# Sliding windows: most loads on GpSimd's queue, tiles cleared by ScalarE, four half-batch stores first

## Chip, cores, metric

One core of one Trainium2 chip. The metric is the device time of one execution in microseconds. The kernel before takes 195.61 us (median of 4 runs).

## The reference

The input x is float32 of shape (16, 64, 64, 64): batch, channels, height, width. Every 8 x 8 window at a stride of 4 is copied out, with all its channels.

```python
n_h = (h - window_size) // stride + 1      # 15
n_w = (w - window_size) // stride + 1      # 15
for i in range(n_h):
    for j in range(n_w):
        result[:, i, j] = x[:, :, i*4 : i*4 + 8, j*4 : j*4 + 8]
```

The output has 16 x 15 x 15 = 3600 rows of 64 x 8 x 8 floats, 16 KB each: 58.98 MB written for 16.78 MB read, and no arithmetic at all.

## The kernel before

A partition of the input tile L holds one band of 16 image rows of one image and of half of the channels: partition = 64 ch + 32 y + 4 b + q, with ch the half of the channels, y the half of the batch, b the image in that half and q the band. A load brings one (ch, y, q): 8 partitions, four apart, each with 32 channels x 4 KB. VectorE and ScalarE gather windows from L into one of four tiles G of 128 output rows, and GpSimd scatters a tile to the output with row numbers from an index tile. Numbers out of range skip a row: a "half store" has the rows of one half of the batch (64), a "whole" store 128, a "crossing" store (windows across two bands) 112.

```python
    L = lpool.tile([P, CL, RB, W], f32)
    x_v = x.rearrange("(y b) (ch cl) (hq r) w -> ch y hq b cl (r w)", y=NY, ch=CH, hq=HQ)
    SMALL = 4

    def load(eng, ch, y, q, c0, c1):
        p0 = ch * HP + y * QP + q
        eng.dma_start(out=L[p0 : p0 + QP - HQ + 1 : HQ, c0:c1, :, :], in_=x_v[ch, y, q, :, c0:c1, :])

# ... index tiles idx, idx_y0, idx_y1, idx_lo, idx_hi (VectorE, small) ...

    for y in range(NY):
        for q in range(HQ):
            load(nc.sync, 0, y, q, SMALL, CL)
            load(nc.gpsimd, 0, y, q, 0, SMALL)
            load(nc.gpsimd, 1, y, q, 0, CL)

# ...
    NG = 4
    G = [gpool.tile([P, C, WS, WS], f32, name=f"G{n}") for n in range(NG)]

# ... scatter(g, ix, j, s): indirect store of tile g; fill(g, half, s, j, lo, n, copies): gathers windows ...

    act, dve = nc.scalar.copy, nc.vector.tensor_copy

    EARLY = 3
    assert EARLY < NG
    for t in range(NG):
        for half in range(CH):
            p0 = half * HP + (QP if t < EARLY else 0)
            nc.vector.memset(G[t][p0 : p0 + QP, :, :, :], 0.0)
    t = 0
    for y in range(NY):
        for j in range(EARLY):
            for half in range(CH):
                copies = (dve, dve) if y and half and j == 1 else (act, dve)
                fill(G[t % NG], half, half, j, y * QP, QP, copies)
            scatter(G[t % NG], (idx_y0, idx_y1)[y], j, 0)
            t += 1

    units = [(j, s) for j in range(NW) for s in (0, 2) if s or j >= EARLY]
    for j, s in units:
        g = G[t % NG]
        t += 1
        if s == 0:
            for half in range(CH):
                fill(g, half, s + half, j, 0, HP, (act, dve))
            scatter(g, idx, j, s)
        else:

            turn = j % 2
            fill(g, turn, s, j, 0, HP, (act, act))
            fill(g, 1 - turn, s + 1, j, 0, HP, (dve, dve))
            scatter(g, (idx_hi, idx_lo)[turn], j, s)
```

## Time and profile before

| | before |
|---|---|
| median of 3 runs beside the profile | 195.66 us (195.56 to 195.69) |
| span of the profile | 193.9 us |
| DMA rate while loading / in the steady state | 401 / 421 GB/s |
| last 4 KB load packet ends (packet records) | 47.22 us |
| last output packet ends (packet records) | 190.60 us |

The prediction shows the views it rests on. One more is needed to read the change: the page's table of DMA queues (queue and kind: packets, MB, share of the 16 engines' span).

```profile
q0 software_dynamic: 9616, 68.43, 85.9%
q1 hardware_dynamic: 1856, 7.34, 9.8%
```

The software queue is GpSimd's, the hardware queue is SyncE's. SyncE loads 7.34 MB of the 16.78 MB; of GpSimd's 68.43 MB, 9.44 MB are loads.

### The profile page before, as it was taken

The page shows a single profiled execution, that of the slowest core. Times are in us where ns is not written, and L with a number is a line of the kernel's source. Part 1 is how long each engine was busy: PE and PEld are TensorE (multiplying, and loading weights), DVE is VectorE, ACT ScalarE, POOL GpSimd, SP SyncE. Part 2 cuts the span into 40 slices and gives each one's busy share as a digit, 9 for nine tenths or more (in the row PEclk, how much of TensorE's full clock was granted, in tenths as well). Part 3 has the DMA queues.
Part 4 walks back from the last instruction along what each step waited for, and adds up shares of the span by engine and source line. Part 5 has one row for each costly group of instructions (what it writes and reads, how often), then busy time and mean ns, then how long its engine had stood idle before and what let it go on. Part 6 is the DMA issues. An engine that isn't in the chain of part 4 may idle for free.

```text
span 193.9 us, 478 instructions
## 1 busy us (share of the span) xinstructions
DVE 131.9 (68%) x156; ACT 123.5 (64%) x66; POOL 53.3 (27%) x54
## 2 busy tenths in 40 slices
DVE  6887778995999998766577657774777477643000
ACT  0000008960999999999779677977797779772000
POOL 7402211106463233231404211331323232311000
DMA  2999999999989999999999999999999999999980
GB/s 85 326 408 401 402 399 397 400 400 405 426 333 382 406 419 419 423 423 404 426 433 421 416 419 419 423 423 433 423 416 412 426 423 423 426 416 421 412 345 30
DMA packets 11476, 75.81 MB, mean 391 GB/s; under 512 B 3776, under 2 KB 3776, under 8 KB 7872
## 3 DMA queue, kind: packets, MB, share of 16 engines
q0 software_dynamic: 9616, 68.43, 85.9%
q1 hardware_dynamic: 1856, 7.34, 9.8%
q14 instruction: 4, 0.03, 0.0%
HBM read 16.78 MB, written 69.21 MB: 444 GB/s over the span
## 4 chain that ended last, share of the span: by engine, by line
DMA 66%; DVE 17%; issue 6%; POOL 2%; POOLq 1%; DVEq 0%; PEldq 0%
DMA out_dram<-G,idx 21%; DMA L<-in_x_dram 18%; DMA out_dram<-G,idx_hi 14%; DMA out_dram<-G,idx_lo 12%; DVE G L136 8%; DVE G L139 6%; DVE G L138 3%; POOL L L57 2%; POOLq L204 1%; DVEq L136 0%; POOL pi L68 0%; DVEq L138 0%; PEldq L204 0%
## 5 line engine op out<-in xcount | busy, mean ns | idle before, releaser
L136 ACT COPY G<-L 64x2048 f32<-64x2048 f32 (+1 forms) x65 | 122.2, 1896 | 22.5 <-DMA out_dram<-G,idx 9.9
L136 DVE COPY G<-L 64x2048 f32<-64x2048 f32 (+1 forms) x37 | 44.8, 1221 | 15.6 <-DMA out_dram<-G,idx 12.7
L139 DVE STREAM_SHUFFLE G<-L 64x1024 f32<-64x1024 f32 x30 | 38.3, 1275 | 0.0
L138 DVE COPY G<-L 64x1024 f32<-64x1024 f32 x30 | 20.7, 690 | 20.1 <-DMA out_dram<-G,idx_hi 13.3
L150 DVE MEMSET G<- 32x4096 f32 x8 | 27.8, 3472 | 7.9 <-issue 6.2
L115 POOL DMA_INDIRECT out_dram<-G,idx x12 | 12.4, 1030 | 33.3 <-ACT G L136 33.3
L115 POOL DMA_INDIRECT out_dram<-G,idx_hi x8 | 11.8, 1471 | 31.4 <-DVE G L139 17.8
L136 ACT ACT_TABLE_LOAD x1 | 1.3, 1283 | 29.6 <-DMA L<-in_x_dram 29.6
L57 POOL DMA_DIRECT2D L<-in_x_dram x16 | 9.8, 626 | 25.0 <-DMA L<-in_x_dram 24.4
L115 POOL DMA_INDIRECT out_dram<-G,idx_lo x7 | 9.7, 1390 | 20.5 <-ACT G L136 14.3
L115 POOL DMA_INDIRECT out_dram<-G,idx_y x6 | 9.3, 1547 | 13.7 <-DVE G L136 8.8
L77 DVE TENSOR_TENSOR th<-tc,tq 128x1 int32<-128x1 int32 x2 | 0.3, 159 | 0.1
L77 DVE CUSTOM_DVE_ANT_0 idx_y<-idx,th 128x2 uint16<-128x2 uint16 x2 | 0.3, 158 | 0.1
L74 DVE TENSOR_SCALAR th<-tc 128x1 int32<-128x1 int32 x2 | 0.3, 154 | 0.1
L68 POOL IOTA pi<- 128x1 int32 x1 | 0.1, 125 | 0.4 <-PEq L204 0.4
L139 DVE LOAD_MASK_SELECT G<-L x30 | 0.2, 6 | 0.0
L77 DVE CUSTOM_DVE_ANT_0 idx_hi<-idx,th 128x2 uint16<-128x2 uint16 x1 | 0.2, 159 | 0.0
L77 DVE CUSTOM_DVE_ANT_0 idx_lo<-tb,th 128x2 uint16<-128x2 uint16 x1 | 0.2, 159 | 0.0
L77 DVE CUSTOM_DVE_ANT_0 idx<-tb,th 128x2 uint16<-128x2 uint16 x1 | 0.2, 161 | 0.0
L77 DVE CUSTOM_DVE_ANT_0 idx_lo<-idx_lo,th 128x2 uint16<-128x2 uint16 x1 | 0.2, 158 | 0.0
L77 DVE CUSTOM_DVE_ANT_0 tb<-tb,th 128x2 uint16<-128x2 uint16 x1 | 0.2, 159 | 0.0
L91 DVE TENSOR_SCALAR th<-th 128x1 int32<-128x1 int32 x1 | 0.2, 153 | 0.0
(13 smaller groups left out, 1.7 us busy)
## 6 DMA issues: line engine op xcount, KB each, us to landing
L<-in_x_dram POOLq DMA_DIRECT2D x8, 1024.0 KB, 21.1
L<-in_x_dram SPq DMA_DIRECT2D x8, 896.0 KB
L<-in_x_dram POOLq DMA_DIRECT2D x8, 128.0 KB, 21.3
out_dram<-G,idx POOLq DMA_INDIRECT x12, 14.6
out_dram<-G,idx_hi POOLq DMA_INDIRECT x8, 13.9
out_dram<-G,idx_lo POOLq DMA_INDIRECT x7, 14.1
out_dram<-G,idx_y POOLq DMA_INDIRECT x6, 6.2
```

Source lines behind the costliest of these rows:

```text
L57: eng.dma_start(out=L[p0 : p0 + QP - HQ + 1 : HQ, c0:c1, :, :], in_=x_v[ch, y, q, :, c0:c1, :])
L68: nc.gpsimd.iota(pi[:, :], pattern=[[0, 1]], base=0, channel_multiplier=1)
L74: nc.vector.tensor_scalar(out=d[:, :], in0=a[:, :], scalar1=float(m), scalar2=None, op0=ALU.mult)
L77: nc.vector.tensor_tensor(out=d[:, :], in0=a[:, :], in1=b[:, :], op=op)
L91: nc.vector.tensor_scalar(out=th[:, :], in0=th[:, :], scalar1=-1.0, scalar2=FAR, op0=ALU.mult, op1=ALU.add)
L115: st = nc.gpsimd.indirect_dma_start(out=o_v, out_offset=bass.IndirectOffsetOnAxis(ap=ix[:, 0:1], axis=0), in_=g.rearrange("p c r w -> p (c ...
L136: copy(out=g[d, cs, :, :], in_=L[f, :, s * ST : s * ST + WS, cols])
L138: copy(out=g[d, cs, 0:ST, :], in_=L[f, :, s * ST : RB, cols])
L139: nc.vector.stream_shuffle(out=g[d, cs, ST:WS, :], in_=L[f, :, 0:ST, cols], mask=nxt)
L150: nc.vector.memset(G[t][p0 : p0 + QP, :, :, :], 0.0)
L204: with _tile.TileContext(nc) as tc:
```

## The change

The intent: with most loads in one queue, the first half of the batch arrives before the second half begins, so that four half stores (one in each tile) can stand in the queue behind the loads. These give 10 us in which the second half of the batch is made ready, and whole stores between its half stores keep the queue full. ScalarE clears the tiles, because it has nothing else to do then.

```diff
--- before.py
+++ after.py
@@ -50,7 +50,8 @@
     x_v = x.rearrange("(y b) (ch cl) (hq r) w -> ch y hq b cl (r w)", y=NY, ch=CH, hq=HQ)
 
 
-    SMALL = 4
+
+    SMALL, HWP = 4, 2
 
     def load(eng, ch, y, q, c0, c1):
         p0 = ch * HP + y * QP + q
@@ -102,8 +103,10 @@
 
     for y in range(NY):
         for q in range(HQ):
-            load(nc.sync, 0, y, q, SMALL, CL)
-            load(nc.gpsimd, 0, y, q, 0, SMALL)
+            hw = y * HQ + q < HWP
+            if hw:
+                load(nc.sync, 0, y, q, SMALL, CL)
+            load(nc.gpsimd, 0, y, q, 0, SMALL if hw else CL)
             load(nc.gpsimd, 1, y, q, 0, CL)
 
     o_v = out.rearrange("b i j c r w -> (b i j) (c r w)")
@@ -142,35 +145,53 @@
 
 
 
-    EARLY = 3
-    assert EARLY < NG
-    for t in range(NG):
+    EARLY = NG
+    zero = ipool.tile([P, 1], f32, name="zero")
+    nc.vector.memset(zero[:, :], 0.0)
+    for g in G:
+        act(out=g.rearrange("p c r w -> p (c r w)"), in_=zero.to_broadcast([P, CFREE]))
+    at = 0
+
+    def tile_():
+        nonlocal at
+        at += 1
+        return G[(at - 1) % NG]
+
+    def part(y, j):
+        g = tile_()
         for half in range(CH):
-            p0 = half * HP + (QP if t < EARLY else 0)
-            nc.vector.memset(G[t][p0 : p0 + QP, :, :, :], 0.0)
-    t = 0
-    for y in range(NY):
-        for j in range(EARLY):
-            for half in range(CH):
-                copies = (dve, dve) if y and half and j == 1 else (act, dve)
-                fill(G[t % NG], half, half, j, y * QP, QP, copies)
-            scatter(G[t % NG], (idx_y0, idx_y1)[y], j, 0)
-            t += 1
-
-    units = [(j, s) for j in range(NW) for s in (0, 2) if s or j >= EARLY]
-    for j, s in units:
-        g = G[t % NG]
-        t += 1
+            fill(g, half, half, j, y * QP, QP, (dve, dve) if y and half else (act, dve))
+        scatter(g, (idx_y0, idx_y1)[y], j, 0)
+
+    crossed = 0
+
+    def unit(j, s):
+        nonlocal crossed
+        g = tile_()
         if s == 0:
             for half in range(CH):
-                fill(g, half, s + half, j, 0, HP, (act, dve))
+                fill(g, half, half, j, 0, HP, (act, dve))
             scatter(g, idx, j, s)
         else:
 
-            turn = j % 2
+            turn = crossed % 2
+            crossed += 1
             fill(g, turn, s, j, 0, HP, (act, act))
             fill(g, 1 - turn, s + 1, j, 0, HP, (dve, dve))
             scatter(g, (idx_hi, idx_lo)[turn], j, s)
+
+    for j in range(EARLY):
+        part(0, j)
+    plain = [(j, 0) for j in range(EARLY, NW)]
+    cross = [(j, 2) for j in range(NW)]
+    for j in range(EARLY):
+        part(1, j)
+        unit(*plain.pop(0))
+    unit(*cross.pop(0))
+    while plain:
+        unit(*cross.pop(0))
+        unit(*cross.pop(0))
+        unit(*plain.pop(0))
 
 
 # ---- launch: one core; inputs and outputs as the reference has them ----
```

## The prediction

> **What bounds the kernel now.** The page comes first: its table of slices shows which resource is full all the way through.
>
> ```profile
> span 193.9 us, 478 instructions
> ...
> DVE 131.9 (68%) x156; ACT 123.5 (64%) x66; POOL 53.3 (27%) x54
> ...
> DMA  2999999999989999999999999999999999999980
> ```
>
> No compute engine is above 68%, and the DMA row is full from the second slice to the last but one. The kernel moves 16.78 MB in and 58.98 MB out (3600 rows of 16 KB), so it is bound by bytes, and only stretches in which the 16 DMA engines are not full, or run at a lower rate, can be won. The view of chosen stretches finds them; the last two columns are the DMA share and GB/s.
>
> ```profile
> 3.00:5.00 2.00, 2.00 (x1) 0.00 (x0) 2.00 (x4) 1.00 0.52 195
> ...
> 12.00:40.00 28.00, 22.93 (x23) 10.36 (x6) 4.27 (x7) 1.00 1.04 401
> ...
> 48.00:54.00 6.00, 5.85 (x5) 5.95 (x4) 3.30 (x2) 1.00 1.03 432
> 54.00:56.00 2.00, 1.94 (x3) 1.98 (x2) 1.35 (x2) 1.00 0.67 271
> 56.00:68.00 12.00, 11.81 (x19) 11.86 (x7) 3.69 (x4) 1.00 0.93 386
> 68.00:180.00 112.00, 75.00 (x97) 91.47 (x49) 31.92 (x25) 1.00 1.01 421
> ...
> 188.00:190.00 2.00, 0.00 (x0) 0.00 (x0) 0.00 (x0) 1.00 0.42 180
> ```
>
> Read downwards: a start at half share (3 to 5 us), loads at 401 GB/s, stores at 432, then a hole at 54 to 56 (share 0.67) and a thin stretch to 68 (0.93), then 112 us at 421 GB/s with nothing missing, and a tail in which the share halves (0.42). The holes are worth (1 - 0.67) x 2 = 0.7 us and (1 - 0.93) x 12 = 0.8 us, 1.5 us together. The timeline of GpSimd says where they come from:
>
> ```profile
> 44.53 1.53 POOL L115 DMA_INDIRECT out_dram<-G,idx_y  x1 [8.77 <-DVE G L136]
> 46.37 1.00 POOL L115 DMA_INDIRECT out_dram<-G,idx_y  x1 [0.31 <-issue]
> 47.67 1.73 POOL L115 DMA_INDIRECT out_dram<-G,idx_y  x1 [0.30 <-issue]
> 52.10 2.20 POOL L115 DMA_INDIRECT out_dram<-G,idx_y  x1 [2.70 <-ACT G L136]
> ```
>
> Three half-batch stores are ready when the loads end (about 47.2 us). Each has 64 rows of 16 KB, 1.05 MB, so 2.5 us at 421 GB/s: the three last to about 54.7. The data of the second half of the batch is there at 48.0 only, so the fourth store is issued at 52.1 and, by the packet records, moves nothing before about 54.8; after it the fills come no faster than ScalarE makes them (two copies of 1.90 us, 3.8 us a tile) until the queue is deep again at 68.
>
> **What the skill says.** (1) "DMA: Bandwidth & Descriptors", section "Why a DMA increments its semaphore by 16 and not by 1": a transfer runs on the largest number of engines up to 16 that divides its slowest dimensions; the hardware queue takes the lowest-numbered ones, the software queue a run of consecutive engines from a round-robin cursor, and all 16 count the semaphore up. Each load here has 8 partitions, so 8 engines. The trace agrees: with SyncE's loads alone in flight (3 to 5 us) the share is about one half, and SyncE's loads report exactly 8 completions each. GpSimd's loads alternate, so its ch=1 loads go to one half of the engines, and SyncE's loads with the small pieces to the other: 8.39 MB on each half. (2) Same page, "Issuing engines are not separate DMA queues": moving a load to another queue gives no bandwidth. The trace agrees: a 4 KB packet takes a median of 164 ns on either queue. (3) "SBUF — State Buffer", "Who interferes with whom": some VectorE modes lock GpSimd out of writing descriptors. Undecided here: GpSimd's first load is issued at 1.48 us, a memset runs from 1.65 to 5.12, and its first 4 KB packet starts at 4.99; but 40 four-byte packets of that queue ran at 2.85, inside that memset. (4) "ScalarE: Activation LUTs", "What ACT_TABLE_LOAD costs": 186 ns + 0.833 ns an element with immediate operands. That gives 1892 ns for 2048 elements, where the trace has 1897.
>
> **The change, part by part.** *Clearing.* Eight memsets of 3.47 us (27.8 us of VectorE before 37 us) go; ScalarE makes four copies of 4096 elements, by (4) 3.6 us each, 14.4 us, after its table load of 1.3 us: done near 18 us. ScalarE now waits for data until 29.6 us, so this is beside other work and costs nothing. What it may give is an earlier first GpSimd packet, at most about 1.5 us on one half of the engines.
>
> *Loads.* SyncE keeps two loads, GpSimd issues the rest, still 16 instructions, still at most eight in flight. The bytes on each half stay 8.39 MB. Two things change. First, loads now arrive in order of the batch: the first half of the batch is 4.19 MB on each half of the engines, four times 1 MB at 5.2 us each (the spacing of the completions of GpSimd's large loads, 11.0, 16.3, 21.4 us), so from about 5.3 us on it lands near 26.5 us and not 29.6. Four fills then need ScalarE for 8 x 1.9 = 15.2 us, to about 42, before the loads end; so four stores (10 us of work), not three, stand right behind the loads. Second, a software load that runs on 8 engines leaves four-byte packets on the other 8. Their count in the records (317 between 14.7 and 20.4 us) is about one per descriptor of one large and one small load. At 7 to 9 ns each they cost 33 x 8 ns = 0.27 us per 1 MB load where nothing else hides them. With six more large software loads interleaved on both halves I estimate up to 6 x 0.23 = 1.4 us longer loading (I take half, 0.7): the half that ends last finishes loading at 47.9 and not 47.2.
>
> *The stores behind them.* Call the end of loading E. The first half store lands at E + 2.6 (in the trace 49.85 for 47.2); only then may its tile be refilled. VectorE's three copies take 3 x 1.22 = 3.65; from GpSimd's issue to the first packet is 2.3 to 2.7 us in the trace (52.10 to about 54.8). So the fifth store moves at E + 8.9, while the four stores ahead of it last to E + 10: no hole on the engines that finished loading last, and up to about 1 us on the half that finished sooner. Whole stores (5.0 us of transfer, 3.8 us of ScalarE) between half stores (2.5 us, 1.9 us of ScalarE) then leave fills faster than transfers, 5.7 against 7.5 us a pair, so the queue gets deeper and the thin stretch to 68 us should vanish.
>
> *The steady state and the tail.* The same 3600 rows at the same rate; two crossing stores per whole one need VectorE 3.9 us against 4.4 us of transfer (112 rows), still under it. The tail stays: eight stores skip 16 rows of one half, seven of the other, so one half has two rows per engine more, 2 x 0.624 = 1.25 us, in both kernels.
>
> *Sum.* The half that ends last moves its first row at 46.7 and its last at about 190.0: 143.3 us for 226 rows per engine. A row takes 0.624 us in the mean, so with its semaphore packets that is 141.6 us of work and 1.7 us of holes. After: restart at E + 8.9 with 16 of the rows done, 210 x 0.6265 = 131.6 us, ends at E + 140.5. With E = 47.2 that is 187.7, a gain of 2.3; with my E of 47.9 it is 188.4, a gain of 1.6. A little of the earlier start (0.2 us) goes on top: 195.66 - 1.8 = 193.9 us.
>
> **The rivals.** *The loads become slower in a single queue.* For: the four-byte packets above, [...]2.8 us from the issue of the first large one to its first packet. Two such loads must be made in the 5.2 us that their transfer takes. Against: eight are in flight, so GpSimd has room. If the full 1.4 us comes and more, the gain is under 1 us: 194.8 to 196. *A new hole takes the place of the old one.* All four tiles are in half stores when the loads end, so nothing can be filled before the first lands; my margin is 1.1 us on one half of the engines and about nothing on the other. A scatter slower by 1 us would give back half of the gain: 194.5 to 195. *The memsets did hold up GpSimd's descriptors.* Then the loads start and end up to 1.5 us sooner, the fifth store with them: 192.2 to 192.7. Reaching under 191.7 needs this and also 4 KB packets at the 159 ns that they took in the first 15 us instead of 164 (256 x 5 ns = 1.3 us more). *Nothing at all*, because the bytes are the same: against it stand the 1.5 us of holes, which the trace shows.
>
> **Range and chances.** All that the trace offers is the 1.5 us of holes, up to 1.5 us at the start and 1.3 us of packet time; all that I can find to lose is about 1.5 us of loading and 1 us of a new hole. So 192.3 to 195.6. Faster by over 2% means below 191.75, which needs nearly all of the gains at once: 0.07. Slower by over 2%, 199.6, needs a stall that nothing here shows: 0.03. Within 2%: 0.90.
>
> **What would show it.** Right: ScalarE's four clears of about 3.6 us over before 20 us; first copies on ScalarE at 26 to 27 us; four half stores issued before 43 us; a DMA share of at least 0.95 between 48 and 68 us; steady state at 421 GB/s as now; first half stores of the second half issued near E + 6.3. Wrong: loads below 395 GB/s or ending after 48.5 us, a hole of over 1 us between 54 and 60, or a first GpSimd load packet near 3.5 us, which would favour the third rival.

## The result

The changed kernel takes 196.94 us (196.88 to 197.19, 4 runs) against 195.61 us. Ratios are the mean time of one kernel's fast runs over that of the other's of the same rounds, so not quite the ratio of the medians: 1.0071, 95% interval 1.0054 to 1.0088. It is slower by 0.7%: the same within 2%, but outside the predicted range of 192.3 to 195.6, and of the other sign than the predicted gain.

| | before | after |
|---|---|---|
| time, median | 195.61 us | 196.94 us |
| ScalarE's wait for the first half of the batch ends | 29.6 us | 26.5 us |
| last 4 KB load packet ends: call it E | 47.22 us | 49.23 us |
| DMA rate while loading (12 to 40 us) | 401 GB/s | 389 GB/s |
| steady state from 66 us | 420 GB/s | 421 GB/s |
| last output packet ends | 190.60 us | 192.14 us |

First the page of the changed kernel, the same queue table. The bytes moved to the software queue as intended, and its packets rose from 9616 to 12448, though the loads are still 4096 packets of 4 KB and the stores 3600 of 16 KB.

```profile
DMA packets 12916, 75.81 MB, mean 388 GB/s; under 512 B 5216, under 2 KB 5216, under 8 KB 9312
...
q0 software_dynamic: 12448, 73.95, 93.0%
q1 hardware_dynamic: 464, 1.84, 2.6%
```

The packets under 512 B rose from 3776 in the kernel before (its page says so) to 5216. They are four bytes long and will matter: 272 of them come with each 1 MB load of GpSimd's queue and 48 with each small one, so six large loads for six small ones make 1344 of the 1440.

Next the stretches of the changed kernel (window, its length, busy time and count of VectorE, ScalarE and GpSimd, clock of TensorE, DMA share, GB/s).

```profile
3.00:5.00 2.00, 0.98 (x7) 2.00 (x1) 2.00 (x4) 1.00 0.53 193
12.00:40.00 28.00, 9.53 (x8) 17.64 (x10) 8.05 (x10) 1.00 1.04 389
...
54.00:56.00 2.00, 1.94 (x3) 1.40 (x2) 0.00 (x0) 1.00 1.03 434
56.00:60.00 4.00, 3.91 (x4) 3.95 (x3) 2.66 (x2) 1.00 0.68 283
60.00:66.00 6.00, 5.84 (x6) 5.93 (x4) 3.46 (x3) 1.00 0.94 393
66.00:180.00 114.00, 84.92 (x113) 93.15 (x50) 32.49 (x27) 1.00 1.01 421
188.00:190.00 2.00, 0.00 (x0) 0.00 (x0) 0.00 (x0) 1.00 0.50 213
190.00:195.40 5.40, 0.00 (x0) 0.00 (x0) 0.00 (x0) 1.00 0.11 46
```

Four readings. The start at half share is as before, although VectorE's memsets are gone. Loading runs at 389 GB/s at a full share of 1.04, so the engines are no less busy, they move less. The hole has moved from 54 to 56 us (share 0.67) to 56 to 60 us (0.68) and is twice as long: (1 - 0.68) x 4 = 1.3 us. And the 0.94 at 60 to 66 us looks like the old thin stretch (0.93 from 56 to 68 us before), but is not. The view counts a packet in the stretch in which it starts. At 59.15 us all 16 engines start again together, so that afterwards 16 packets start together every 0.62 us, and a stretch of 6 us can miss a whole row of them. Over 16 us, or from 61.7 us on, the difference shows (the first line is of the kernel before, the others of the changed one):

```profile
60.00:76.00 16.00, 15.72 (x23) 15.83 (x9) 4.70 (x4) 1.00 0.96 401
...
60.00:76.00 16.00, 14.37 (x12) 11.82 (x7) 9.02 (x6) 1.00 0.99 408
61.70:71.70 10.00, 9.75 (x9) 8.73 (x6) 5.57 (x3) 1.00 1.01 419
```

Reckoned from the time that packets are in flight, cut at the edges of the stretch, the 16 engines idle for 0.7 us in the mean between 60 and 76 us before and for under 0.1 us after; between 50 and 60 us it is 0.55 us before and 1.3 after. So the change did remove the thin stretch, and doubled the hole.

The timeline of the changed kernel, around the same place (start, length, engine, line, operation, tiles, count, and what ended the idle time before):

```profile
41.37 0.96 POOL L118 DMA_INDIRECT out_dram<-G,idx_y  x1 [0.83 <-ACT G L139]
...
52.20 1.90 ACT L139 COPY G<-L 32x2048 f32<-32x2048 f32 x1 [11.11 <-DMA out_dram<-G,idx_y]
52.21 9.99 DVE L139 COPY G<-L 32x2048 f32<-32x2048 f32 x8 [16.09 <-DMA out_dram<-G,idx_y]
...
56.70 1.86 POOL L118 DMA_INDIRECT out_dram<-G,idx_y  x1 [14.37 <-ACT G L139]
```

The fourth half store is issued at 41.37 us, long before the loads end, so the queue is stocked as planned. But then both copy engines stand idle for 11 and 16 us. What they wait for is the landing of the first half store, since all four tiles are in the queue, and that landing comes only at 52.2 us. By the packet records 16 output packets are in flight until 56.5 us, 8 from 57.3 to 58.1, one at 59.0 and 16 again from 59.4. One half of the engines ran dry about 2.2 us before the fifth store came, the other (its last packet ends at 59.04) just before it.

### The profile page after: what moved, and what is told of

It is laid out like the page before. It is cut to its first block, busy times and chain, and to the rows that moved or that the text cites. A ratio compares the mean times of both kernels' runs of the same rounds, so it can differ in the third digit from the quotient of the medians.

```text
span 195.4 us, 465 instructions
## 1 busy us (share of the span) xinstructions
DVE 110.7 (57%) x154; ACT 136.2 (70%) x69; POOL 54.4 (28%) x55
## 3 DMA queue, kind: packets, MB, share of 16 engines
q0 software_dynamic: 12448, 73.95, 93.0%
## 4 chain that ended last, share of the span: by engine, by line
DMA 66%; DVE 16%; issue 5%; POOL 3%; POOLq 1%; DVEq 0%; PEldq 0%
DMA out_dram<-G,idx_hi 42%; DVE G L139 12%; DMA L<-in_x_dram 11%; DMA out_dram<-G,idx_y 8%; DMA out_dram<-G,idx 6%; DVE G L142 3%; POOL L L58 2%; DVE G L141 1%; POOL out_dram L118 1%; POOLq L225 1%; POOLq L118 0%; DVEq L139 0%; DVEq L225 0%; POOL pi L69 0%; DVEq L141 0%
## 5 line engine op out<-in xcount | busy, mean ns | idle before, releaser
L139 ACT COPY G<-L 64x2048 f32<-64x2048 f32 (+1 forms) x64 | 120.8, 1896 | 40.1 <-DMA out_dram<-G,idx_y 11.7
L139 DVE COPY G<-L 64x2048 f32<-64x2048 f32 (+1 forms) x42 | 51.1, 1228 | 47.6 <-DMA L<-in_x_dram 22.4
L118 POOL DMA_INDIRECT out_dram<-G,idx x11 | 13.5, 1230 | 25.4 <-ACT G L139 24.8
L118 POOL DMA_INDIRECT out_dram<-G,idx_y x8 | 10.5, 1313 | 29.1 <-ACT G L139 25.3
L58 POOL DMA_DIRECT2D L<-in_x_dram x16 | 11.5, 723 | 16.9 <-DMA L<-in_x_dram 16.4
L118 POOL DMA_INDIRECT out_dram<-G,idx_lo x7 | 6.7, 960 | 29.4 <-DVE G L142 21.7
L152 ACT COPY G<-zero 128x4096 f32<-128x4096 f32 x4 | 14.1, 3600 | 0.0
```

Source lines behind the costliest of these rows:

```text
L118: st = nc.gpsimd.indirect_dma_start(out=o_v, out_offset=bass.IndirectOffsetOnAxis(ap=ix[:, 0:1], axis=0), in_=g.rearrange("p c r w -> p (c ...
L139: copy(out=g[d, cs, :, :], in_=L[f, :, s * ST : s * ST + WS, cols])
L152: act(out=g.rearrange("p c r w -> p (c r w)"), in_=zero.to_broadcast([P, CFREE]))
```

## The experiments

In the text below "the half that SyncE serves" is the eight engines that take ch=0 loads, the other half those that take ch=1 loads. The packet records have no engine numbers; the halves are told apart by the completions, which come in groups of eight. The diffs below are cut. E is always the end of the last 4 KB load packet in the packet records of the profiled run.

### Loads put back (e1_loads_back)

```diff
-    SMALL, HWP = 4, 2
+    SMALL, HWP = 4, 8
```

> The changed kernel with the loads of before (eight on SyncE, small and large ones alternating on GpSimd). Theory (loads): the four-byte packets that 8-engine software loads leave on the other 8 engines lengthen the loading by about 2 us on the half that ends last (49.2 to 47.3), and the first refill waits for that half. So here the load rate is back at 400 GB/s, the first copy after the loads starts near 50.1 instead of 52.2, and the time falls by about 2 us, to 194.9 (194.3 to 195.4), under the kernel before. Rival (order and tiles): four half stores in four tiles leave none to fill when the loads end, whatever the loads do; the time stays at 196.3 to 197.2. Rival (arrival order): the first half of the batch lands later (29.6 instead of 26.5), the four half stores come late, and the time is over 197.

Measured: 195.15 us (195.01 to 195.42, 5 runs), ratio to the kernel before 0.9978 (0.9964 to 0.9991). E is 47.35 us and the copies for the fifth store start at 50.29 us.

```profile
12.00:40.00 28.00, 9.38 (x8) 14.48 (x8) 6.63 (x8) 1.00 1.04 401
54.00:56.00 2.00, 1.94 (x3) 1.98 (x2) 1.21 (x1) 1.00 1.03 434
56.00:60.00 4.00, 3.91 (x4) 3.95 (x3) 2.51 (x2) 1.00 0.94 385
60.00:66.00 6.00, 5.84 (x6) 4.81 (x4) 3.72 (x2) 1.00 0.94 393
```

The load rate is back at 401 GB/s and the hole is much smaller (0.94 for 0.68; by the packets in flight, 0.4 us of idle time between 50 and 60 us instead of 1.3). The theory of the loads held within 0.3 us (195.15 for 194.9); the order of the stores alone is not at fault, and the later arrival of the first half of the batch (29.7 us) does no harm that shows. The 0.94 at 60 to 66 us is again the way of counting: over 60 to 76 us the share is 0.99.

### Loads of the changed kernel alone (e2_loads_only)

```diff
-            load(nc.sync, 0, y, q, SMALL, CL)
-            load(nc.gpsimd, 0, y, q, 0, SMALL)
+            hw = y * HQ + q < HWP            # HWP = 2, in the kernel before
+            if hw:
+                load(nc.sync, 0, y, q, SMALL, CL)
+            load(nc.gpsimd, 0, y, q, 0, SMALL if hw else CL)
             load(nc.gpsimd, 1, y, q, 0, CL)
```

> The kernel before with the loads of the changed one alone (two on SyncE). Theory (loads): loading at 388 GB/s, the second half of the batch is there at 49.9 instead of 48.0, the fourth store is issued near 54.0 instead of 52.1, and the time rises by about 1.9 us to 197.5 (197.0 to 198.0), ratio 1.007 to 1.012. Rival (loads harmless, order to blame): 195.3 to 195.9, because the bytes are the same and the first half arrives earlier.

Measured: 197.08 us (196.89 to 197.18, 5 runs) against 195.65, ratio 1.0070 (1.0056 to 1.0084), E = 49.14 us. The loads alone cost 1.4 us, as much as the whole change. The detail of the issue was missed: the fourth store is issued early, at 51.93 (54.0 expected), because ScalarE could begin its copies at 47.83, when one half of the channels was there, and the fifth late, at 56.58.

### Clears alone (e3_clears_only)

```diff
-    for t in range(NG):
-        for half in range(CH):
-            p0 = half * HP + (QP if t < EARLY else 0)
-            nc.vector.memset(G[t][p0 : p0 + QP, :, :, :], 0.0)
+    zero = ipool.tile([P, 1], f32, name="zero")
+    nc.vector.memset(zero[:, :], 0.0)
+    for g in G:
+        act(out=g.rearrange("p c r w -> p (c r w)"), in_=zero.to_broadcast([P, CFREE]))
```

> The kernel before with its tiles cleared by ScalarE alone. Theory: no effect, 195.4 to 195.9: the clears run beside the loads on either engine, and the first 4 KB packet of GpSimd's queue started at 4.99 us in both kernels. Rival (memsets hold up GpSimd): 194.3 to 195.2.

Measured: 195.96 us (195.76 to 195.99, 5 runs) against 195.65, ratio 1.0010 (0.9997 to 1.0024): no difference that can be told from zero (the median lies 0.06 us above the expected 195.4 to 195.9). The rival that the memsets held up GpSimd is out; the first 4 KB packet of its queue started at 4.90 us without them.

### Sixteen engines per load (e4_sixteen_engines)

```diff
+    x_w = x.rearrange("b (ch cl) (hq r) w -> ch hq b cl (r w)", ch=CH, hq=HQ)
+    for q in range(HQ):
+        for ch in range(CH):
+            p0 = ch * HP + q
+            nc.gpsimd.dma_start(out=L[p0 : p0 + HP - HQ + 1 : HQ, :, :, :], in_=x_w[ch, q])
```

(in place of all loads of the changed kernel)

> A diagnosis, not a candidate: the changed kernel with all loads on GpSimd as eight transfers of 16 partitions (both halves of the batch in one), so that each runs on all 16 engines and leaves no other half. Theory (four-byte packets): few four-byte packets during loading, about 405 GB/s (398 or more) between 12 and 40 us, loads over near 46.6 us. Rival (a software queue alone is slower than two queues): 389 GB/s as in the changed kernel, loads over near 48.3. The time itself is worse by about 10 us, since the first fill waits for all loads.

Measured: 236.79 us, one run, correct. Neither theory foresaw what happened:

```profile
12.00:70.00 58.00, 0.00 (x0) 4.15 (x2) 0.00 (x0) 1.00 1.03 207
```

The load rate is half, at a full share: a 4 KB packet takes a median of 332 ns instead of 161 in the changed kernel. The Trainium skill has the reason, and I had not applied it: "SBUF — State Buffer", section "Door 1: The DMA port swizzle", says that partitions 0 to 63 reach only 8 of the 16 ports, and so do 64 to 127. A load of one ch writes to one of these halves; sixteen engines then share eight ports. The trace agrees: 207 GB/s, where the page gives 218 as the limit of 8 ports. The run says nothing on the four-byte packets, and the theory needed another test. It fits the way this kernel always has one ch=0 load and one ch=1 load side by side.

### Four loads on SyncE (e5_four_on_sync)

```diff
-    SMALL, HWP = 4, 2
+    SMALL, HWP = 4, 4
```

> The changed kernel with four loads on SyncE instead of two (all of the first half of the batch), so four large software loads fewer than six meet others on the half of the engines that ends last. Theory (four-byte packets): each large load replaced by a small one takes away 28 packets of 8 ns, 0.22 us; two of them 0.45 us; loading ends at 48.8 instead of 49.2 and the time is 196.5 (196.2 to 196.8). Within the run the load rate is near 401 GB/s while both queues load (12 to 24 us) and near 388 when only the software queue does (30 to 42 us). Rival (order of arrival matters, not the count): no change from the changed kernel, 196.9, or a jump to the 195.2 of eight loads on SyncE.

Measured: 196.39 us (196.34 to 197.02, 6 runs), ratio 1.0047 (1.0034 to 1.0060), E = 48.41 us. In one run, first with both queues loading, then with the software queue alone:

```profile
12.00:24.00 12.00, 0.00 (x0) 4.15 (x2) 2.62 (x4) 1.00 1.04 405
30.00:40.00 10.00, 5.93 (x6) 9.98 (x7) 2.62 (x3) 1.00 1.04 384
```

The time was foreseen to 0.1 us (196.5 expected), E was not (48.8 expected; 0.3 us of the difference is a first load that ended at 11.70 us and not at 12.00). The time lies between two and eight loads on SyncE, and the rate falls within the run when SyncE's loads are over. The first half of the batch arrives as in the changed kernel (26.3 us), so it is the number of large software loads that counts, and not the order of arrival.

### Rows of 16 KB (e6_long_rows), wrong result on purpose

```diff
-        eng.dma_start(out=L[p0 : p0 + QP - HQ + 1 : HQ, c0:c1, :, :], in_=x_v[ch, y, q, :, c0:c1, :])
+        dst = L[p0 : p0 + QP - HQ + 1 : HQ, c0:c1, :, :].rearrange("p (k four) r w -> p k (four r w)", four=4)
+        eng.dma_start(out=dst, in_=x_l[ch, y, q, :, c0 // 4 : c1 // 4, :])   # x_l: whole channels, 16 KB each
```

> A diagnosis with a wrong result on purpose: the changed kernel with the same loads, engines, queues and bytes, but each reads rows of 16 KB from other channels (four times fewer descriptors, so four times fewer four-byte packets, 9 instead of 33 per large load). A 16 KB packet takes 0.618 us in the stores, so eight of them 4.94 us. Theory (four-byte packets): one large load follows another on a half of the engines after 4.94 + 9 x 0.008 = 5.02 us (5.42 in the changed kernel, of which 5.17 is data). Rival (a software queue loses a fixed 0.25 us per load): 4.94 + 0.25 = 5.19 us.

Measured: the completions of the large loads on one half follow each other at 29.50, 34.47, 39.46, 44.43 and 49.40 us, 4.98 us apart. In the changed kernel they are 5.43 us apart (for instance 33.67, 39.10 and 44.53). With the same number of loads, queue and engines, the loss per load (over the data time of 5.17 and 4.94 us in the expectation) fell from 0.25 to about 0.05 us when there were a quarter of the descriptors. So it is not a fixed cost per load. A cost for each descriptor elsewhere, in the making of them for instance, would fall in the same way; that it is the four-byte packets rests on their count and length in the records, and on the spacing of the loads shown below. The rate of this stretch:

```profile
24.00:40.00 16.00, 5.17 (x5) 5.27 (x3) 5.28 (x7) 1.00 1.01 423
```

A software queue alone can load at 423 GB/s. The time of this run, 201.77 us, means nothing: SyncE's second load ended only at 24.1 us, and from 12 to 24 us the rate was 275 GB/s.

### Three half stores first, then whole ones (e7_three_first)

```diff
-    EARLY = NG
+    EARLY = 3
     # loads of before (HWP = 8); of the second half, whole stores first;
     # the last loop stops when no crossing store is left
-        part(1, j)
         unit(*plain.pop(0))
+        part(1, j)
```

> The changed kernel with the loads of before, three first half stores instead of four, then whole and half stores in turn, whole first. Theory (no tile is free when the loads end): with three, the fourth tile is filled from about 48 us without waiting for a store to land, the next store is issued near 52.7 and moves near 55.0 against an empty queue at 54.2 to 54.7; being whole it gives 5 us for the next, so the thin stretch (0.94 between 60 and 66 us) goes: 194.6 (194.2 to 195.0). Rival (four in the queue are worth as much as the free tile): 195.15 as with the loads alone put back.

Measured: 195.45 us (195.30 to 195.75, 5 runs), ratio 0.9994 (0.9981 to 1.0006). The theory fell: a free tile gives nothing. The copies did start at 48.3 us without waiting for a landing, but only 7.5 us of stores stand in the queue, and the hole came at 54 to 56 us (share 0.54). A free tile moves the refill forward by about as much (2 us) as the missing half store shortens the queue (2.5 us).

### A small piece first (e8_early_start)

```diff
+    smalls = [(0, 0, 0, 2), (0, 0, 2, SMALL)] + [(y, q, 0, SMALL) ... the other seven]
+    larges = [(0, 0, 0, SMALL), (0, 0, SMALL, CL)] + [(y, q, 0, CL) ... the other seven]
+    for (y0, q0, a0, a1), (y1, q1, b0, b1) in zip(smalls, larges):
+        load(nc.gpsimd, 0, y0, q0, a0, a1)
+        load(nc.gpsimd, 1, y1, q1, b0, b1)
```

> The changed kernel with the loads of before, and the first large software load cut so that a piece of four channels goes first. Theory (the half of the engines that SyncE does not serve starts at 5.0 us because the first large load takes 2.8 us from issue to its first packet): its first packet comes near 3.4, the share between 3 and 5 us rises from 0.52 to 0.8 or more, this half ends loading 1 to 1.5 us sooner, the other then ends last near 46.8, and the time falls by 0.3 to 0.6 us to 194.7 (194.4 to 195.0). Rival (something else holds the software queue until 5 us): no change, 195.15.

Measured: 195.20 us (195.17 to 195.50, 5 runs), the same as with the loads put back, E = 47.32 us. The first 4 KB packet of the software queue came at 4.90 us and the share from 3 to 5 us is 0.52. My reason for the late start, the length of the first large load's descriptor list, is wrong.

### No load on SyncE (e9_none_on_sync), and a whole store first (e10_none_whole_first)

```diff
-    SMALL, HWP = 4, 2
+    SMALL, HWP = 4, 0
```

and, for the second run only, besides:

```diff
-        part(1, j)
         unit(*plain.pop(0))
+        part(1, j)
```

> The changed kernel with no load on SyncE: all sixteen large loads on GpSimd. Every large load now leaves 33 four-byte packets on the other half, eight times 5.43 us of loading on each half. In the sixteen-partition run, without SyncE, GpSimd's first 4 KB packet came at 2.92 us; with SyncE's loads it came at 4.9 to 5.0 in every run. Theory A (SyncE's first loads hold up GpSimd's first packets): both halves start near 3.0 to 3.4 and end loading together near 46.6 to 47.0; the first copies after the loads start near 49.7 and the time is 194.6 (194.2 to 195.1), although the four-byte packets are at their most. Theory B (fewer loads on SyncE is worse, whatever else): start at 5.0, loading ends at 48.5 or later on both halves, 196.5 to 197.3.

> The run above with whole and half stores of the second half of the batch in turn, but a whole one first. Theory (the thin stretch at 60 to 66 us comes from a half store of 2.5 us that stands alone in the queue): a whole store takes the same 3.8 us to fill and lasts 5.0, so the share between 60 and 66 us rises from 0.94 to 0.98 or more, and the time falls by 0.3 to 0.5 us against the run above: 194.2. Rival (the hole after the four half stores sets the loss): no difference between the two runs.

Measured: 197.18 us (197.07 to 197.24) and 197.10 us (197.04 to 197.23), 5 runs each, ratios 1.0075 and 1.0074, E = 49.37 and 49.25 us. Theory A fell and B held for the time, though not in detail: one half did start at 3.06 us and end before 48.5. Without SyncE the first packet comes at 3.06 us, but on one half of the engines only:

```profile
3.00:5.00 2.00, 0.98 (x7) 2.00 (x1) 2.00 (x5) 1.00 0.52 144
12.00:40.00 28.00, 9.53 (x8) 17.51 (x10) 7.70 (x10) 1.00 1.04 388
```

The other half still starts near 5 us. Why the second software load never moves data before that stays open. The half that SyncE served ends its loads at 48.1 us by its semaphores, 0.3 us later than in the changed kernel (47.8), the other half 0.1 us later by E, and the time is 0.2 us longer: too close together to tell which half sets the time. And a whole store first changes nothing; the stretch that it was to fill was not thin (see The result).

### Seven and two channels moved to the other half (e11_shift_seven, e12_best_shift_two)

```diff
-            load(nc.gpsimd, 1, y, q, 0, CL)
+            last = (y, q) == (NY - 1, HQ - 1)
+            load(nc.gpsimd, 1, y, q, 0, CL - 7 if last else CL)
+            if last:
+                load(nc.gpsimd, 1, y, q, CL - 7, CL)
```

(and with 2 for 7 on top of the loads put back)

> The changed kernel with its last large load cut in two, so that its last seven channels go, by the round-robin cursor, to the half of the engines that has done loading first. In the runs so far the time is the end of loading on the later half plus 147.7 to 148.0 us (196.94 with 49.23, 195.15 with 47.35, 196.39 with 48.41, 197.18 with 49.37). Theory (the later half alone sets the time, because the first refill waits for a store that needs both halves): seven packets of 0.162 us move, 1.13 us from the later half to the earlier, both end near 48.1 to 48.3, and the time is 195.9 (195.6 to 196.2). Rival (the total of loading work sets it): no change, 196.9.

> The best kernel so far (loads of before in the changed kernel, 195.15) with two channels of its last large load moved in the same way to the other half. Theory: the later half ends 0.3 us sooner, 47.05, and the time is 194.9 (194.6 to 195.2), which would be the best of the study. Rival: one more load in the queue costs as much as it saves, 195.15 to 195.4.

Measured: 197.08 us (197.04 to 197.34) and 195.55 us (195.42 to 195.64), 5 runs each, ratios 1.0078 and 0.9994. Both missed, because E did not fall: 49.00 us instead of 48.1 to 48.3, and 47.69 instead of 47.05. The stretch in which the piece moves shows why:

```profile
46.00:48.00 2.00, 0.00 (x0) 0.00 (x0) 0.00 (x0) 1.00 1.17 338
```

338 GB/s at a share above one: now both halves of the engines write to the partitions of ch=1 at once, as in the run with sixteen engines, and the 4 KB packets from 47 to 48 us take a median of 308 ns, instead of 159 in the changed kernel. The equalisation could not be had in this way. The relation between E and the time holds in these runs too: E + 148.1 and E + 147.9.

A fifth tile, which would end the wait for a landing, was not run: five tiles need 80 KB per partition beside the 128 KB of L. It was found not to fit.

## Why the prediction was wrong

**The bound and the holes before: right.** The kernel is bound by bytes in both forms, at 420 and 421 GB/s in the steady state, and ScalarE's clears cost nothing that can be measured.

**The stocking of the queue: right.** The first copies run at 26.5 us (26 to 27 predicted), and four half stores are issued by 41.4 us (43 predicted). **The thin stretch "should vanish": right.** The share is 0.99 between 60 and 76 us, for 0.96 before. (A whole and a half fill take 6.3 us together, from the scatter at 56.70 us to the one at 62.96, and not 5.7: VectorE's five copies of 1.23 us are longer than ScalarE's three.)

**The step that failed: "I estimate up to 6 x 0.23 = 1.4 us longer loading (I take half, 0.7)".** Loading got longer by 2.0 us: E went from 47.2 to 49.2, where I had put 47.9. The mechanism was named and its count was right (33 packets of 7 to 9 ns per 1 MB load), but I halved it without a reason in the trace. Nothing hides these packets. On the later half the large loads complete at 12.00, 17.36, 22.79, 28.24, 33.67, 39.10, 44.53 and 49.67 us: 5.36 to 5.45 us apart as long as a burst of four-byte packets follows, and 5.14 for the last, behind which none comes. In the kernel before they are 5.15 apart in the mean (11.44 to 47.49). So six bursts cost 1.6 us, 0.27 each, the 33 x 8 ns of the prediction in full. The first load ended 0.56 us later; with the loads put back it ended at 11.73, so part of this is scatter. Together that is 2.2 us by the completions, where the packet records have 2.0. Two loads fewer of this kind gave back 0.55 us, six gave back 1.8, and long rows removed the loss.

**The second miss: "the fifth store moves at E + 8.9".** It moved at 59.15, E + 9.9. The landing came at 52.2, E + 2.95 for E + 2.6. (The prediction took 49.85 us from the kernel before, but that is the eighth of the store's 16 completions; the last comes at 50.30, E + 3.1.) The copies took 3.7 us, but the scatter was issued 0.8 us after the last copy, a term that I did not have, and its first packet came 2.4 us after that. This miss does not hang on the loads: with them put back the fifth store moves at 57.25, again E + 9.9.

**The third: "210 x 0.6265 = 131.6 us" for the rows after the restart.** On the half that ends last they took 132.4 us (59.15 to 191.53, leaving out one last row of a single engine, as the prediction's 190.0 does). One half is also slower by row: the completions of the last store come at 188.4 us from one half and from 191.4 from the other (187.8 and 190.1 before), 3.0 us apart, where the tail's two rows make 1.25. Why is open.

The sum, for the profiled run of 197.19 us: 1.3 us from E, 1.0 from the restart, 0.8 from the rows and 0.2 from an earlier start that did not come make 3.3, which is the distance from 193.9. It is bookkeeping in the prediction's own terms, with all of these but E untested one by one. The loads are 1.3 of it: with them put back the prediction's sum gives about 193.3 us, and 195.15 was measured.

Of the signs of being wrong that the prediction named, three came: loads below 395 GB/s (389), an end after 48.5 us (49.2) and a hole of over 1 us between 54 and 60 (1.3).

**Where the expected gain went.** The end of loading is paid in full, whatever the stocked queue: the table below shows it. The traces show the chain. The first refill needs a store that has landed, and a landing needs both halves of the engines. In all eight kernels of the table the fifth store's first packet comes 9.90 to 9.99 us after E, and then all 16 engines start again within 0.2 us. So the later half starts the chain, while the earlier half has 10 us of stores from its own, earlier end. In the changed kernel the first half store's completions come at 49.6 to 50.3 us from one half and at 51.3 to 52.2 from the other, a lag of 1.7 to 1.9 us, and the earlier half was dry for 2.2 us before the fifth store. On the later half the four stores last to 59.04, E + 9.8, so a quicker chain could have served the earlier half only. Which half ends the kernel, and so what that would have been worth, the records do not tell; no run changed one half alone. In all eight timed kernels with four half stores first, the median time is E plus 147.7 to 148.1 us:

| kernel | E, us | time, us | time - E |
|---|---|---|---|
| changed | 49.23 | 196.94 | 147.7 |
| loads put back | 47.35 | 195.15 | 147.8 |
| four on SyncE | 48.41 | 196.39 | 148.0 |
| small piece first | 47.32 | 195.20 | 147.9 |
| none on SyncE | 49.37 | 197.18 | 147.8 |
| none, whole first | 49.25 | 197.10 | 147.9 |
| seven moved | 49.00 | 197.08 | 148.1 |
| two moved, loads put back | 47.69 | 195.55 | 147.9 |

The kernel before lies at 148.4 (47.22 and 195.66). The run with the loads alone, which has three half stores first, lies at 147.9 (49.14 and 197.08), so the table does not show that the four stores are what sets the difference.

**The parts.** The loads cost 1.4 us alone and 1.8 us in the changed kernel (196.94 - 195.15, from two sessions); the clears 0.3 us at most, not distinct from zero; the four half stores and the new order gain 0.8 us with the loads of before (195.15 against 195.96 with the clears alone; 0.5 against the kernel before), but with the loads of the change next to nothing (196.94 against 197.08 with the loads alone, with ranges that overlap). It is the order that removed the thin stretch: with the loads alone the engines still idle for 0.7 us between 60 and 76 us. Of my rivals, the first ("The loads become slower in a single queue", 194.8 to 196) was the right one, at a larger size, together with the second, a new hole in place of the old. The third, the memsets, was wrong.

The best version is the changed kernel with the loads put back: 195.15 us, 0.22% faster than before (0.09 to 0.36%).

Open: why the second software load moves no data before about 5 us, why one half of the engines is slower by row, and which half ends the kernel.

## What to carry to other kernels

Before moving transfers to another queue, count its descriptors on every engine and not only its bytes: here a software load on 8 engines also occupied the other 8, and a term that was seen was halved by feeling. When a buffer is freed by a store that all engines share, the slowest of them sets the refill, however well the others are stocked (E + 9.9 us in eight kernels). A measured cost per item should go into a sum whole, unless a line of the trace shows what hides it. A share that counts packets by their start misleads in a stretch of a few packets' length: here it showed a hole that was not there.

## What the Trainium skill lacked or had wrong

- "DMA: Bandwidth & Descriptors", section "Why a DMA increments its semaphore by 16 and not by 1", says that all 16 engines count up for a software transfer, but not that the engines without data also get a four-byte packet per descriptor: 272 of them in a burst per 1 MB load of 8 x 32 descriptors, 7 to 9 ns each, 389 GB/s instead of 401 while loading; with rows of 16 KB, and so a quarter of the descriptors, 423.
- "SBUF — State Buffer", section "Can I just issue two DMAs to hit both halves?", answers no, they serialize. Two loads on 8 engines each, one to partitions below 64 and one to those above, ran side by side at 401 GB/s here, while loads on 16 engines to one such half ran at 207 (as its section "Door 1: The DMA port swizzle" has it).
- No page has the late start of the second software transfer: issued at 2.2 us, it moved no data before about 5 us (4.8 to 5.1), with or without SyncE's loads, VectorE's memsets, or a long list of descriptors ahead.
- "SBUF — State Buffer", section "Who interferes with whom", has the conflict of VectorE's copies with GpSimd's descriptor writing, but no size for an indirect store. What is seen here fits it, without an experiment of its own: a scatter spans 0.96 to 1.05 us on GpSimd while VectorE has nothing to do and 1.86 beside its copies (of the changed kernel, at 36 to 42 and at 56 to 74 us).
